# A two-layer hybrid encoder on one core: ScalarE, VectorE and GpSimd pinned to the written order in the attentions, with late work, straddling value blocks and fill rewritten

## The chip, the core and the metric

The kernel runs on one core of a Trainium2 chip. The metric is the device time of one execution in microseconds. A core has five engines that work side by side and meet at semaphores: TensorE (PE: matmuls and transposes into PSUM), VectorE (DVE), ScalarE (ACT), GpSimd (POOL) and SyncE (SP, which here issues all transfers). PEld stands for TensorE's weight loads.

## The reference

Two layers over 512 tokens (a grid of 8 rows by 64 columns) of width 1024, each with three residual parts, all in float32:

```python
x = x + hybrid_mixer(rms_norm(x, norm_mix[l]), ...)
x = x + memory_cross_attention(rms_norm(x, norm_mem_q[l]), rms_norm(mem, norm_mem_kv[l]), ...)
x = x + conv_ffn(rms_norm(x, norm_ffn[l]), ...)
```

The mixer projects its input once into two groups of heads of width 64. Eight heads do neighbourhood attention (NA) in a window of 8 rows by 16 columns with a learned relative bias. Eight query heads with two key-value heads do grouped attention (GQA) over all tokens, after a per-head RMS norm of q and k and an axial rotation. Both outputs go through one output projection. The memory attention has 4 heads of width 128 over 256 memory tokens. The feed-forward part is a SwiGLU (inner width 2816) with a depthwise convolution of width 3 over the positions. A last RMS norm closes the program.

## The kernel before

**Data.** Activations are kept transposed, 128 channels by 512 tokens (`xT`, eight chunks). Every operand of a large product is split into a high part `hi` and a rest `lo`, and a product is three matmuls (`mm3`). Weights arrive in float32 by SP (`emit_raw`, three buffers); ACT writes `hi` (L246) and POOL `lo` (L247), for up to three weights ahead of use, at the moment `get_w` asks for the next weight.

**Order.** The program is written in Tile. TensorE and SP are pinned to the order in which the program writes their instructions (`keep_in_program_order`, which ties an instruction to the one written before it on its engine). ACT, DVE and POOL are wrapped in `Free`, which passes calls through, so the order of their instructions is left to the framework's scheduler.

**Fill.** `weave` writes an attention as a software pipeline: in step s it writes the transposes of unit s-2, the normalise of unit s-1, the scores of unit s, and so on, and between them calls the filler. `Filler.run(ns)` adds `ns` to an account and takes the next pieces of a list of generators until their TensorE time (by a formula in `Counted.matmul`) has used it up. The list holds, in order: projections of the NA heads, of the GQA heads (`gqa_project`, order k, 0, 1, v, 2, 3), the NA half of the output projection (`out_na`), memory keys, memory values 0, and `close_rows("outg")`, the GQA half of the output projection, which has the memory values 1 as a generator `between`. A generator may yield a gate, a condition that must hold before it goes on; what is left at the end is written by `finish`. NA has 8 units (a pair of heads, half of the queries each) with three fills a step; GQA has 16 units with one fill a step.

**Late work.** `late(n, fn)` keeps `fn` until n ticks later. A tick comes after every filler piece, and also when a generator ends. So an eviction that needs time is written behind later matmuls.

**The rotary units.** After its projection each of k, 0, 1, 2, 3 is scaled and squared by ACT (L768, L769) and multiplied by the cosine table on DVE (L770). Two ticks later `rotate` writes four transfers that swap rows, POOL's product and sum (L775, L776), TensorE's sums of squares into a `tr` bank, DVE's scaling (L781, L783) and POOL's power and copy (L784, L785). Three ticks later `norm` spreads the factors by TensorE (`mm<-ident,t`), multiplies on DVE (L792) and splits the result (ACT L620, DVE L622). `gqa_v` turns v by four transposes (`turn`) two ticks after its projection.

**The other lines.** `split_psum` evicts a bank as `hi` (ACT L441) and `lo` (DVE L442). POOL normalises the exponentials (L448) with DVE's reciprocal (L825 in GQA); ACT's exponentials are L674 and L819, DVE's maxima L817. NA's values are folded by L718 to L720 and split by `split_out` (ACT L463, POOL L464) into `parts[0..3]`; GQA's values are folded by `fold` (ACT L455, DVE L457, then ACT L458 and POOL L459) into `parts[4..7]`, and `whole[i]` opens the gates of `close_rows`. `mem_stat` and `memory_prepare` write the memory's statistics (DVE L504) and operands (ACT L488, DVE L489) at the start of some GQA steps. `project_v` also writes value blocks that straddle two token blocks, by two ACT copies for each of three blocks (L642, L643). PSUM has four `mm`, two `sc` and two `tr` banks.

## Time and profile before

| | us |
|---|---|
| three runs | 1452.25, 1452.06, 1448.22 (median 1452.06) |
| the profiled execution, its own time | 1450.3 |
| its span from the first to the last instruction | 1448.4 |
| TensorE busy | 1375.9 |
| VectorE / ScalarE / GpSimd busy | 846.3 / 720.1 / 706.3 |
| mean granted TensorE clock | 0.977 |

How to read the profile: an instruction has the line of `kernel.py` that wrote it; pinned instructions have the line of the helper (L76 for matmuls, L63 for transposes and transfers). A tile's name stands without its number: `tr`, `sc` and `mm` are PSUM banks, `r` the general operand buffers, `t` temporary tiles, `xg` the large operand pair, `raw`, `hi`, `lo` weights. "x8" counts instructions. A wait is named by what ended last before the waiting instruction. By the timeline, layer 0's NA steps run to about 158 us, its GQA steps to about 280, its memory attention to about 360; layer 1's GQA steps run from about 867 to 987 and its memory attention to about 1060.

### The profile page before, as it was taken

Reading aid. Unit: us, or ns where it says so; the run is one execution under the profiler, and the core shown is the slowest. Engines: PE = TensorE matmul, PEld = TensorE weight load, DVE = VectorE, ACT = ScalarE, POOL = GpSimd, SP = SyncE. Lnnn points to the kernel's source line nnn. Section 1 sums busy time; section 2 is a strip of 40 time slices with the busy share of each in tenths; the row PEclk is TensorE's granted clock in tenths of the full one; section 3 lists DMA queues with packets and bytes.
Section 4 is the critical chain, followed back from the end, with each engine's and each line's share of the span. In section 5 each row is a group of like instructions: output and inputs, shape, how many; then the busy total and the mean of one; then the engine's idle time right before and its main releaser. Section 6 shows DMA issues by size and latency. Waiting matters only on the chain. (4 is left out here: it accounts for less than half of the span.)

```text
span 1448.4 us, 19205 instructions
## 1 busy us (share of the span) xinstructions
PE 1375.9 (95%) x7092; PEld 1173.4 (81%) x7092; DVE 846.3 (58%) x1437; ACT 720.1 (50%) x1332; POOL 706.3 (49%) x509
## 2 busy tenths in 40 slices
PE   7998799899999999999999987989899999999997
PEld 6987689677888888888888876987788888888897
DVE  5666566446488258448446646754637862871874
ACT  5785557556444234324557754756554432431441
POOL 2457547453544444444645655646254444444451
PEclk8999899899999999999999998999999999999998
DMA  7353212221333333332354432222223333333321
GB/s 231 117 140 94 73 44 74 71 75 53 94 95 96 102 93 91 104 104 81 106 151 140 109 90 68 69 59 88 58 59 107 97 102 92 96 89 105 96 77 59
DMA packets 216573, 135.68 MB, mean 94 GB/s; under 512 B 5664, under 2 KB 210720, under 8 KB 216480
## 3 DMA queue, kind: packets, MB, share of 16 engines
q1 hardware_dynamic: 216480, 134.46, 32.1%
q8 instruction: 56, 0.92, 0.3%
q14 instruction: 37, 0.30, 0.1%
HBM read 125.00 MB, written 2.10 MB: 88 GB/s over the span
## 5 line engine op out<-in xcount | busy, mean ns | idle before, releaser
L247 POOL TENSOR_TENSOR lo<-raw,hi 128x1024 fp32r<-128x1024 f32 (+2 forms) x268 | 500.2, 1878 | 575.0 <-ACT hi L246 558.7
L76 PE MATMUL mm<-xg,hi 128*128 128x512 f32 x1984 | 620.7, 394 | 1.9 <-ACT xg L63 1.5
L76 PEld LDWEIGHTS mm<-xg,hi 128*128 128x128 f32 x1984 | 372.8, 190 | 77.9 <-ACT xg L63 1.9
L246 ACT CAST hi<-raw 128x512 fp32r<-128x512 f32 (+2 forms) x276 | 224.1, 836 | 338.7 <-PE mm L76 290.5
L76 PE MATMUL mm<-xg,lo 128*128 128x512 f32 x992 | 388.7, 392 | 0.0
L76 PE MATMUL mm<-r,hi 128*128 128x512 f32 (+1 forms) x1160 | 341.3, 378 | 15.7 <-ACT r L458 12.1
L76 PEld LDWEIGHTS mm<-r,hi 128*128 128x128 f32 x1160 | 213.4, 191 | 57.5 <-ACT r L458 12.9
L1096 DVE SCALAR_TENSOR_TENSOR t<-t,par,t 128x7 f32<-128x7 f32 (+1 forms) x352 | 203.9, 647 | 34.0 <-ACT t L1089 34.0
L76 PEld LDWEIGHTS mm<-xg,lo 128*128 128x128 f32 x992 | 188.1, 190 | 40.3 <-DVE lo L247 0.4
L76 PE MATMUL mm<-r,lo 128*128 128x512 f32 (+1 forms) x580 | 217.9, 376 | 0.0
L76 PEld LDWEIGHTS mm<-r,lo 128*128 128x128 f32 x580 | 110.4, 190 | 19.3
L448 POOL TENSOR_SCALAR t<-t,s 128x512 f32<-128x512 f32 (+1 forms) x112 | 66.3, 607 | 97.2 <-DVE s L825 59.1
L1081 DVE TENSOR_TENSOR t<-mm,rep 128x512 f32<-128x512 f32 x88 | 60.2, 687 | 77.6 <-PE mm L76 62.3
L1098 ACT ACTIVATE t<-t 128x512 f32<-128x512 f32 x44 | 27.9, 633 | 138.9 <-DVE t L1096 138.9
L1102 DVE TENSOR_TENSOR r<-t,r 128x512 fp32r<-128x512 f32 x44 | 90.4, 2055 | 7.3 <-ACT r L1101 4.1
L1125 DVE TENSOR_TENSOR xT<-xT,mm 128x512 f32<-128x512 f32 x32 | 21.9, 686 | 106.7 <-PE mm L76 106.7
L63 PE MATMUL tr<-ident,t 128*128 128x128 f32 x456 | 65.5, 284 | 17.1 <-DVE r L442 11.5
L76 PE MATMUL sc<-r,r 128*128 128x256 f32 (+1 forms) x352 | 74.8, 345 | 3.4 <-DVE r L442 1.8
L63 PEld LDWEIGHTS tr<-ident,t 128*128 128x128 f32 x456 | 55.8, 147 | 23.5 <-issue 17.1
L1089 ACT ACTIVATE t<-t,par 128x512 f32<-128x512 f32 x88 | 66.8, 806 | 2.4 <-DVE t L1081 2.4
L76 PE MATMUL mm<-r,r 128*128 128x256 f32 (+1 forms) x428 | 62.2, 297 | 0.0
L76 PEld LDWEIGHTS sc<-r,r 128*128 128x128 f32 x352 | 53.6, 196 | 9.6 <-ACT r L441 3.0
(135 smaller groups left out, 1551.9 us busy)
## 6 DMA issues: line engine op xcount, KB each, us to landing
raw<-in_w_up SPq DMA_DIRECT2D x88, 512.0 KB, 3.9
raw<-in_w_in SPq DMA_DIRECT2D x34, 512.0 KB, 4.5
raw<-in_w_down SPq DMA_DIRECT2D x32, 448.0 KB, 3.9
raw<-in_w_mem_kv SPq DMA_DIRECT2D x16, 512.0 KB, 3.8
raw<-in_w_down SPq DMA_DIRECT2D x16, 512.0 KB, 4.2
r<-in_bias SPq DMA_DIRECT2D x16, 384.0 KB, 5.2
r<-r SPq DMA_DIRECT2D x18, 256.0 KB, 3.7
raw<-in_w_out SPq DMA_DIRECT2D x8, 512.0 KB, 3.8
```

Source lines behind the costliest of these rows:

```text
L63: return lambda *a, **k: self.tc.keep_in_program_order(op(*a, **k))
L76: return self.tc.keep_in_program_order(self.engine.matmul(out, lhsT, rhs, **k))
L246: act.copy(hi[:, k], raw[:, k])
L247: (POOL if eng[0] == "P" else DVE).tensor_sub(lo[:, k], raw[:, k], f(hi)[:, k])
L448: eng.tensor_scalar(e, e, sums[:, col : col + 1], 1.0, op0=ALU.mult, op1=ALU.mult)
L1081: DVE.tensor_mul(u, us[side], ffn.rep)
L1089: ACT.activation(cc, u, AF.Identity, bias=par[:, l, CB + ch : CB + ch + 1], scale=w[1])
L1096: DVE.scalar_tensor_tensor(cc[:, dst], u[:, src], wi, cc[:, dst], op0=ALU.mult, op1=ALU.add)
L1098: ACT.activation(cs[0], cs[0], AF.Silu)
L1102: DVE.tensor_sub(acts[j][1], cs[0], f(acts[j][0]))
L1125: DVE.tensor_add(xT[m], xT[m], pm)
```

## The change

- `Free` becomes `Switched`: while `ordered[0]` holds, every instruction of ACT, DVE and POOL is pinned to the written order as well. The switch is off at the start of layer 0, turned on after the first fill pieces there (in layer 1 from the layer's start), and off again before each feed-forward part.
- `Filler.run` ticks once when it finds the gate closed, and `finish` ticks until the gates open.
- `fold` and `split_out` write their last two instructions one tick later, and `whole` or `parts` is set then; `out_na` waits for `parts[3]`.
- `rotate` is cut in two: `swap`, one tick after the projection (transfers, sums of squares, DVE's scaling), and `rotate`, one tick later (POOL: power, copy, product, sum); `norm` follows two ticks after that.
- The straddling blocks of v are written by five transfers on SP for each half of v, two ticks after its last block, in place of twelve ACT copies a layer.
- `close_rows` writes the first of memory values 1 ahead of the gate of the third chunk, and the rest behind the gate of the last chunk. Memory values 1 splits one weight less ahead.
- The GQA fill is 2300 in sixteen steps and 3000 in the last four.

```diff
--- before.py
+++ after.py
@@ -46,7 +46,7 @@
 
 
 NA_FILL = 2650
-GQA_FILL = [2950] * 16 + [3000, 3000, 3000, 2900]
+GQA_FILL = [2300] * 16 + [3000] * 4
 MEM_FILL = [1, 1, 1, 2, 1, 0, 0, 2, 0, 1, 2]
 MEM_STEPS = [1, 0, 1, 1, 1, 1, 1, 1, 1] + [0] * 11
 N_RAW, N_W, AHEAD, AHEAD_HELD, N_WARM, N_LATE, N_FIRST = 3, 4, 2, 5, 10, 4, 3
@@ -76,14 +76,18 @@
         return self.tc.keep_in_program_order(self.engine.matmul(out, lhsT, rhs, **k))
 
 
-class Free:
-
-
-    def __init__(self, engine):
-        self.engine = engine
+class Switched:
+
+
+
+    def __init__(self, tc, engine, ordered):
+        self.tc, self.engine, self.ordered = tc, engine, ordered
 
     def __getattr__(self, name):
-        return getattr(self.engine, name)
+        op = getattr(self.engine, name)
+        if self.ordered[0]:
+            return lambda *a, **k: self.tc.keep_in_program_order(op(*a, **k))
+        return op
 
 
 class PartsView:
@@ -141,14 +145,18 @@
 
     def run(self, ns):
         self.owed += ns
+        if self.closed():
+            self.late.tick()
         while self.owed > 0 and not self.closed():
             t = self.pe.ns
             self.step(1)
             self.owed -= self.pe.ns - t
 
     def finish(self):
-        self.step(1 << 30)
-        assert not self.gens
+        while self.gens:
+            assert not self.closed() or self.late.todo
+            self.late.tick()
+            self.step(1 << 30)
         self.late.flush()
 
 
@@ -171,7 +179,8 @@
     PE, SP = Counted(tc, nc.tensor), InOrder(tc, nc.sync)
     late = Late()
     ACT_IN_ORDER = InOrder(tc, nc.scalar)
-    ACT, DVE, POOL = Free(nc.scalar), Free(nc.vector), Free(nc.gpsimd)
+    ordered = [False]
+    ACT, DVE, POOL = [Switched(tc, e, ordered) for e in (nc.scalar, nc.vector, nc.gpsimd)]
 
     cpool = ctx.enter_context(tc.tile_pool(name="cpool", bufs=1))
     xpool = ctx.enter_context(tc.tile_pool(name="xpool", bufs=1))
@@ -247,10 +256,10 @@
             (POOL if eng[0] == "P" else DVE).tensor_sub(lo[:, k], raw[:, k], f(hi)[:, k])
         ready.append((hi, lo))
 
-    def get_w(key):
+    def get_w(key, ahead=AHEAD):
         n = done[0]
         assert plan[n][0] == key, (plan[n][0], key)
-        ahead = n + 1 + AHEAD
+        ahead = n + 1 + ahead
         while ahead < min(len(plan), n + 1 + AHEAD_HELD) and plan[ahead][4][1:] == "r":
             ahead += 1
         while len(ready) < min(len(plan), ahead):
@@ -447,7 +456,7 @@
     def normalise(e, sums, col, eng=DVE):
         eng.tensor_scalar(e, e, sums[:, col : col + 1], 1.0, op0=ALU.mult, op1=ALU.mult)
 
-    def fold(out, po, cs):
+    def fold(out, po, cs, done):
 
         th, o32 = tmp((2, 256)), tmp((256,))
         rows = [slice(64 * j, 64 * j + 64) for j in range(2)]
@@ -455,8 +464,13 @@
             ACT.copy(th[r, j], po[64:128, j])
         for j, r in enumerate(rows):
             DVE.tensor_add(o32[r], po[0:64, j], th[r, j])
-        ACT.copy(out[0][:, cs], o32)
-        POOL.tensor_sub(out[1][:, cs], o32, f(out[0][:, cs]))
+
+        def split():
+            ACT.copy(out[0][:, cs], o32)
+            POOL.tensor_sub(out[1][:, cs], o32, f(out[0][:, cs]))
+            done()
+
+        late(1, split)
 
     def split_out(o32):
         hi, lo = rpair()
@@ -637,11 +651,19 @@
                     mm3(pm, xg[k][0][:, bs], xg[k][1][:, bs], wh, wl, k == 0, k == KC - 1)
                 v = vblk[g][P * b]
                 split_psum(v[:, :, 0:HD], v[:, :, HD:P], pm.rearrange("p (h d) -> p h d", d=HD), mix.rstd[:, b : b + 1])
-                if b > 0:
-                    o = vblk[g][P * b - 64]
-                    ACT.copy(o[0:64], vblk[g][P * b - P][64:128])
-                    ACT.copy(o[64:128], v[0:64])
+                if b == NB - 1:
+                    late(2, lambda: straddle(vs))
                 yield
+
+        def straddle(vs):
+            for dst, src in (
+                (vs[2][0:64, 0:2], vs[0][64:128, 0:2]),
+                (vs[2][64:128, 0], vs[0][0:64, 1]),
+                (vs[2][64:128, 1], vs[1][0:64, 0]),
+                (vs[3][0:64, 0], vs[1][64:128, 0]),
+                (vs[3][64:128, 0], vs[1][0:64, 1]),
+            ):
+                SP.dma_start(f(dst), f(src))
 
 
         na = {}
@@ -719,7 +741,7 @@
                 DVE.tensor_add(tt[r], po[0:64], th[r])
             DVE.tensor_add(o32s[p][:, 256 * bp : 256 * bp + 256].rearrange("p (i q) -> p i q", i=2), tt[:, :, 0], tt[:, :, 1])
             if bp == 1:
-                parts[p] = split_out(o32s.pop(p))
+                late(1, lambda: parts.__setitem__(p, split_out(o32s.pop(p))))
                 bias[p] = None
                 del qk["q", p], qk["k", p]
                 if p % 2 == 1:
@@ -769,21 +791,26 @@
             ACT.activation(sq, pm, AF.Square)
             DVE.scalar_tensor_tensor(cc, pm, gain, gtab[0][:, 0], op0=ALU.mult, op1=ALU.mult)
 
-            def rotate():
+            def swap():
                 for i in range(4):
                     SP.dma_start(xr[32 * i : 32 * i + 32], xs[32 * (i ^ 1) : 32 * (i ^ 1) + 32])
-                POOL.tensor_mul(xr, xr, gtab[0][:, 1])
-                POOL.tensor_add(xr, cc, xr)
                 pv = ps_t()
                 for b in range(NB):
                     PE.matmul(pv[:, 2 * b : 2 * b + 2], sq[:, b * P : (b + 1) * P], pairs, start=True, stop=True)
-                v, r = small(2 * NB), small(2 * NB)
+                v = small(2 * NB)
                 DVE.tensor_tensor(v.rearrange("p (b j) -> p b j", j=2), pv[:, 0 : 2 * NB].rearrange("p (b j) -> p b j", j=2),
                                   r2[0].unsqueeze(2).to_broadcast([P, NB, 2]), op=ALU.mult)
+
                 DVE.tensor_scalar(v, v, *((1.0 / HD, EPS) if g == "k" else (1.0, EPS * HD)), op0=ALU.mult, op1=ALU.add)
+                late(1, lambda: rotate(v))
+
+            def rotate(v):
+                r = small(2 * NB)
                 POOL.tensor_tensor(r, v, mhalf[:, : 2 * NB], op=ALU.pow)
                 POOL.tensor_copy(sq.rearrange("p (b d) -> p b d", d=HD), r.unsqueeze(2).to_broadcast([P, 2 * NB, HD]))
-                late(3, norm)
+                POOL.tensor_mul(xr, xr, gtab[0][:, 1])
+                POOL.tensor_add(xr, cc, xr)
+                late(2, norm)
 
             def norm():
                 pr = ps_mm()
@@ -797,7 +824,7 @@
                     gq[g] = rtile((2, S))
                     split_q(pr, gq[g])
 
-            late(2, rotate)
+            late(1, swap)
 
 
         ga, gpt = {}, {}
@@ -859,10 +886,10 @@
             del gpo[u], gpt[u // 2]
             if bp == 0:
                 parts[4 + i] = rpair()
-            fold(parts[4 + i], po, slice(256 * bp, 256 * bp + 256))
-            whole[i] = bp == 1
+            fold(parts[4 + i], po, slice(256 * bp, 256 * bp + 256), lambda: whole.__setitem__(i, bp == 1))
 
         def out_na():
+            yield lambda: parts[3] is not None
             for m in range(KC):
                 if m % 2 == 0:
                     w = get_w(("outn", m // 2))
@@ -885,12 +912,15 @@
                 rows.append((ps_mm(), w[m // 2], slice(P * (m % 2), P * (m % 2) + P)))
                 gemm_T(*rows[m][:2], ops, range(2), 0, 3, rows[m][2])
                 yield
+            for _ in range(len(between) and 1):
+                next(between[0])
+                yield
             yield lambda: ready(2)
             for pm, ws, c in rows:
                 gemm_T(pm, ws, ops, [2], 0, 3, c)
+            yield lambda: ready(3)
             for gen in between:
                 yield from gen
-            yield lambda: ready(3)
             norm = norm()
             for m in range(KC):
                 if m < n:
@@ -922,7 +952,7 @@
         def memory_values(g):
             if g == 0:
                 memv.extend(rpair() for _ in range(MB))
-            w = [get_w(("memv", g, kh)) for kh in range(2)]
+            w = [get_w(("memv", g, kh), AHEAD - g) for kh in range(2)]
             for b in range(MB):
                 pm = ps_mm()[:, :256]
                 bs = slice(b * P, b * P + P)
@@ -935,6 +965,7 @@
 
         if l > 0:
             load_bias(0)
+        ordered[0] = l > 0
         units = [project_v(p) if n == "v" else project_qk(n, p) for n, p in NA_ORDER]
         nns = []
         attn_fill = Filler(
@@ -943,6 +974,7 @@
             close_rows("outg", 2, PartsView(parts, 4), lambda k: whole[k], lambda: nns.append(Norm(G_MQ, l)) or nns[0],
                        memory_values(1)))
         attn_fill.step(N_FIRST if l == 0 else N_FIRST + 5)
+        ordered[0] = True
 
         def na_quanta(s):
             if s == 3:
@@ -1046,6 +1078,7 @@
         fill.finish()
 
 
+        ordered[0] = False
         ffn = nn
         acts = {}
 
```

## The prediction

> **What bounds the kernel now.** I read the page first, then who TensorE waited for, then TensorE's timeline at each wait, then the same microseconds on every engine. The profiled execution took 1450.3 us (span 1448.4 and 1.9 around it), 1.8 below the median of 1452.06; the sum below is made against 1450.3. About 0.3% (4.4 us) is what a measurement of this kernel can tell from no change.

> ```profile
> PE 1375.9 (95%) x7092; PEld 1173.4 (81%) x7092; DVE 846.3 (58%) x1437; ACT 720.1 (50%) x1332; POOL 706.3 (49%) x509
> ...
> PE   7998799899999999999999987989899999999997
> ...
> PEclk8999899899999999999999998999999999999998
> ```

> TensorE is the bound: the kernel can only gain where it stands still or runs at a low clock. Both happen in the same slices, 4 to 9 and 23 to 28, which are the attentions of the two layers; the feed-forward part is full.

> ```profile
> PE mm L76 <- ACT r L458: 12.1, 4, 3.8
> PE tr L63 <- DVE r L442: 11.5, 2, 5.8
> ...
> PE tr L76 <- DVE s L825: 6.8, 1, 6.8
> PE mm L76 <- POOL t L785: 6.4, 3, 3.7
> PE tr L63 <- DVE s L825: 4.7, 1, 4.7
> ```

> Columns: total us, times, longest. Two places per layer hold nearly all of it. The **tail** of the grouped attention (L458, the folded output): idle 3.85+0.26+0.34+2.21 = 6.7 us in layer 0 and 7.3 in layer 1. The **transition** from the neighbourhood attention to the grouped one (L442, L785, L825): 0.79+5.76+1.01+2.48+6.76+0.39 = 17.2 in layer 0, 0.47+5.75+0.20+3.70+4.74 = 14.9 in layer 1.

> ```profile
> 145.00:184.00 39.00, 28.74 (x134) 24.00 (x133) 23.05 (x37) 18.96 (x38) 21.89 (x20) 0.85 0.28 79
> 184.00:257.00 73.00, 72.56 (x480) 66.15 (x480) 48.39 (x94) 51.06 (x119) 44.11 (x50) 0.98 0.22 63
> 257.00:283.00 26.00, 19.32 (x111) 16.54 (x110) 7.94 (x16) 10.36 (x24) 8.56 (x9) 0.80 0.18 52
> ```

> Windows of layer 0 (start:end, length, busy of PE, PEld, DVE, ACT, POOL, then the granted clock): transition, steady grouped attention, tail. The steady part is full at 5.6 us a step (transposes at 214.96, 220.58, 226.22), so the tail is idle only because its fill was spent earlier.

> The transition's longest wait, all engines:

> ```profile
> 136.11 2.54 POOL L247 TENSOR_TENSOR lo<-raw,hi 128x512 fp32r<-128x512 f32 x2
> ...
> 138.60 1.26 POOL L776 TENSOR_TENSOR t<-t,t 128x512 f32<-128x512 f32 x1
> ...
> 140.54 0.69 DVE L792 TENSOR_TENSOR mm<-t,mm 128x512 f32<-128x512 f32 x1
> 141.27 1.17 ACT L620 CAST r<-mm 64x512 fp32r<-64x512 f32 x2 [1.93 <-DVE mm L792]
> ...
> 142.47 1.39 DVE L622 TENSOR_TENSOR r<-mm,r 64x512 fp32r<-64x512 f32 x2 [1.24 <-ACT r L620]
> 143.89 1.29 DVE L442 TENSOR_TENSOR r<-tr,r 128x512 fp32r<-128x512 f32 x2
> ...
> 144.73 1.09 PE L63 MATMUL tr<-ident,t 128*128 128x128 f32 x4 [5.76 <-DVE r L442]
> ```

> A transpose waits for a `tr` buffer, which DVE empties only after the rotary product L792, which waits for POOL's add L776, which stood behind a weight split (L247). The chain starts at POOL. After a wait TensorE is also slow: from 144.73 four transposes and twelve matmuls take 5.6 us, against 3.1 later, so 2.5 us lost; after the 2.48 wait 1.6, after 6.76 2.0. Layer 1 likewise: 2.5, 1.7, 1.2. Clock in the transitions: 11.5 us. In the tail, six matmuls from 261.04 take 3.1 us against 1.37, and again from 279.75: 3.4 lost; layer 1 some 1.8.

> **Part 1, the tail.** Walking the filler's account through the code (227 ns for a 512-column matmul, 120 for 256) shows steps 17 and 18 of the old grouped weave without fill, as the trace has it. With 2300 a step the fill reaches the end: step 16 holds the second block of memory values 0, step 17 two first halves of `outg` rows, step 18 a block of memory values 1, step 19 the third chunk of the rows; then the last block (24 matmuls, 2.88 us) stands between the last fold and the closing rows. The fold's chain is 2.95 us in the trace (L455 at 275.22 to the end of L459 at 278.14); over it now lie 1.36+2.88 = 4.2 us. The fill is only moved: the earlier steps shorten to about 5.0 us. Removed: 6.7+3.4+7.3+1.8 = 19.2; I leave 0.5 a layer, so 18.2. If the cover were gone it would cost 2.2 again in each layer.

> **Part 2, the transition.** DVE, ACT and POOL now run in the written order. A rotary unit (5 a layer) costs POOL power 1.65, copy 0.61, product 1.29, sum 1.28 = 4.8 us, a weight split 2.54, a normalise 1.4. From the split written with unit 0 to the first grouped transpose POOL has 5x2.54 + 2.54 for the first `outn` + 4x4.8 + 1.3 for each of three outputs + 4x1.4 = about 44 to 50 us (by whether the first rotary unit's end counts); TensorE has 49 us there. Both are full, so each wait in the fixed order shows. I lay the new order out by hand with these rows:
> - The statistics of a unit are now written right at the next fill call, and its squares (ACT L768 0.69, L769 0.59) must be ready: 1.35 us after the projection, behind a 0.9 us piece: 0.45 wait once; for unit 2 nothing lies between: 1.4.
> - The norm of unit 1 comes one half projection after its rotation was written. POOL has in front of it the split of v's weights and `split_out` (2.54+1.3): the copy is about 3.0 late (0.45 for unit 0).
> - The transpose after `turn` waits for L442 behind L622, as before, but POOL's four operations are now together: about 1.5 instead of 5.8.
> - At the first grouped step the written order is: scores 0, norm of unit 2, split of output 3, statistics of unit 3, rotation of unit 3, weights, `outn` half, normalise 0, scores 1, `outn` half, norm of unit 3, transposes 0. ACT reaches the split of output 3 only after two exponentials (0.69 each) that wait for DVE's L770 and maxima, and after L620 (1.18): about 5.4 us after scores 0. The second `outn` half waits 1.7 for it, norm 3 waits 1.7 for POOL's copy, and the transposes wait for POOL's 1.3+4.8+2.5+1.4 = 10 us, of which TensorE covers half: 5.0.

> Sum 0.45+0.45+3.0+1.5+1.4+1.7+1.7+5.0 = 15.2 a layer, 30.4 in both, clock (1.6+2.3 a layer) 7.8: 38.2 against 32.1+11.5 = 43.6. Gain 5.4. Next late is POOL. Bounds: 3 us of waits a layer (POOL never idle) to 20; I take the laid-out value, which is nearest to the 17.2 and 14.9 of now. DVE's memory reductions (2.06 each, part of the old 6.76) fall into the 5.0 wait and cost nothing; without it they would cost up to 2.5.

> **Part 3, the shorter steps.** ACT is busy 39.2 of 52 us from 198 to 250, DVE 37.0, POOL 31.6. At 5.0 instead of 5.6 us a step this is 85%, 80% and 68%: still room, but POOL's normalise now stands behind the weight split of the step before, and steps with one short `outn` half (4.2 us) leave no slack. I take 1 us in each of three such steps: +3 a layer, 6 in both. Bounds 0 and 20.

> A row that bears on this: the memory operands' L489 (two a step, written ahead of the transposes in four steps a layer) has a median of 0.475 us, but five of its sixteen took 0.87 to 1.49, each beside a POOL instruction; 3.2 us of DVE in all, off the path, so I add nothing. [...]

> **Part 4, at nothing.** Twelve ACT copies a layer at 0.62 become ten transfers (about 0.6 us of issue each on SP, 128 to 256 KB). The first reader comes some 9 us of TensorE work later; the 256 KB copies among `r` tiles land in 3.7 us (the page's median), five in a row, 0.6 apart, in about 6.5 (an estimate from these rows). Behind them on SP stand weight loads three ahead, and the swap. If the cover were gone: up to 3 us each. ACT's 7.4 us a layer lie where TensorE is full. The memory attention (idle 4.2 us a layer) is pinned but not rewritten: 0, bounds -1 and +3 a layer.

> **Sum.** 1450.3 - 18.2 - 5.4 + 6 = 1432.7, say 1433; its own range 1418 to 1445 (part 2 with 11 to 18 us of waits a layer, part 3 with 0 to 12 in both).

> **Rivals.** (a) **The transition clears**: POOL runs without holes and the waits fall to 3 a layer, no new ones in the steady steps. For it: POOL stood 11 us idle inside the old stall (139.9 to 151.0). Against: the hand-laid order has two holes of 4 to 5 us. Waits 6 instead of 30.4, clock 0, steady 0: 1433 - 24 - 8 - 6 = 1395. (b) **The pinned queues cost more than they give, slower**: in the grouped steps POOL's normalise (L448) queues behind the weight split (2.54) with about 0.9 of slack, so 1.7 us in each of some ten steps a layer that write a split, 34 in all instead of 6: 1433 + 28 = 1461. It decides from 23.6 us, the gain of parts 1 and 2, which is 0.7 us in each of the 32 grouped steps. For it: ACT at 85%; against: the split falls into the fill, which is longest just there (2.88). [...] (c) **No net effect**: the transition at its upper bound (20 of waits and 5 of clock a layer, +12) and three more slow steps a layer (+6) take back what the tail gives: 1433 + 18 = 1451.

> **Numbers.** Forecast 0.53, (a) 0.24, (b) 0.15, (c) 0.08. Faster is the forecast and (a), 0.77; same takes most of (c), 0.07; slower 0.16. The range 1392 to 1458 leaves out the far half of (a) and of (b), some 0.1 each.

> **What would show it.** Right: no wait of the closing rows for the last folded output over 0.5 us, step length about 5.0 up to the end; a wait of about 5 us of the first grouped transposes for POOL's normalise; no 5.8 us wait for L442. (a): those are gone as well. (b): waits for the normalise of 1 to 2 us spread over the grouped steps, clock dips inside them. Wrong: idle TensorE in the neighbourhood steps before the first rotary unit (ACT or DVE blocked behind a weight's landing or a straddling block), or in the memory attention above 5 us a layer.

## The result and the profile after

The changed kernel takes 1514.66 us (median of 1508.98 to 1517.57) against 1452.12 us for the kernel before on the same chip. The ratio is 1.0431, with a 95% interval of 1.0412 to 1.045: slower by 62.5 us, where 1433 us and a gain were forecast. The time lies 57 us above the upper end of the range. The profiled execution took 1517.57 us (span 1515.8).

The page first: busy time of the engines, then PE and the granted clock in 40 slices.

```profile
PE 1407.5 (93%) x7092; PEld 1190.1 (79%) x7092; DVE 848.5 (56%) x1437; ACT 705.4 (47%) x1308; POOL 705.2 (47%) x509
...
PE   8988889897999999999999978989799999999997
...
PEclk9998999998999999999999988999989999999998
```

TensorE has the same 7092 matmuls as before, but is busy 31.6 us longer (1407.5 against 1375.9) and idle 35.8 us longer (108.3 against 72.5). The sum, 67.4, is the difference of the spans. So about half of the loss is waiting. Most of the other half is the low clock behind the waits: the mean granted clock is 0.961 over 1515.8 us against 0.977 over 1448.4, which makes some 26 us more lost to the clock; the remaining 6 us of longer busy time are not accounted for. The loss lies in the attentions: the last stretch, from layer 1's feed-forward part to the end, takes 358 us in both.

From the first and last score matmul of each attention, the stages of layer 0 compare so (layer 1 in brackets): first neighbourhood score to first grouped score 113.9 to 133.0 us (113.8 to 133.3); grouped scores 98.2 to 95.1 (95.7 to 92.2); last grouped score to first memory score 60.7 to 62.9 (59.3 to 61.9); memory scores 21.5 to 30.7 (21.5 to 30.5); last memory score to the feed-forward part 46.9 to 53.5 (46.7 to 53.5). The loss is in the neighbourhood stage with the transition, and in the memory attention.

Whom TensorE waited for (total us, times, longest), to be read beside the five rows of before:

```profile
PE tr L63 <- POOL t L89: 25.8, 14, 3.2
PE tr L63 <- DVE t L89: 21.4, 8, 4.5
PE tr L63 <- DVE s L89: 11.2, 2, 5.6
PE mm L76 <- POOL t L89: 7.1, 2, 3.6
PE tr L76 <- DVE r L89: 7.0, 4, 1.8
PE tr L76 <- ACT t L89: 3.5, 4, 1.3
PE mm L76 <- POOL lo L89: 3.3, 4, 1.4
```

L89 is the helper that keeps an instruction in order, so every ordered instruction has this line. The row of the folded output (12.1 us) is gone. In its place the closing rows wait 1.4 us a layer for a weight's low part (the last row above, longest 1.4). The two large new rows, 25.8 and 21.4 us, are transposes that wait for a normalise, by GpSimd in the mixing attentions and by VectorE in the memory attention. I show four of these waits.

**Memory attention, 4.48 us.** All engines, layer 0 (start, us, then idle time before it and its releaser):

```profile
352.05 0.46 ACT L89 ACTIVATE t<-sc,s 128x256 f32<-128x256 f32 x1
...
352.50 0.58 ACT L89 CAST r<-mm 128x512 fp32r<-128x512 f32 x1
353.11 0.69 DVE L89 TENSOR_TENSOR r<-mm,r 128x512 fp32r<-128x512 f32 x1 [1.56 <-ACT r L89]
353.72 0.69 DVE L89 SCALAR_TENSOR_TENSOR mm<-mm,rep 128x512 f32<-128x512 f32 x1
354.44 0.58 ACT L89 CAST r<-mm 128x512 fp32r<-128x512 f32 x1 [1.36 <-DVE mm L89]
354.93 0.59 ACT L89 CAST r<-tr 128x512 fp32r<-128x512 f32 x1
355.06 0.69 DVE L89 TENSOR_TENSOR r<-mm,r 128x512 fp32r<-128x512 f32 x1 [0.65 <-ACT r L89]
355.67 0.68 DVE L89 TENSOR_TENSOR r<-tr,r 128x512 fp32r<-128x512 f32 x1
356.27 0.15 DVE L89 RECIPROCAL s<-s 128x2 f32<-128x2 f32 x1
356.46 0.62 DVE L89 TENSOR_SCALAR t<-t,s 128x256 f32<-128x256 f32 x2
356.96 0.66 PE L63 MATMUL tr<-ident,t 128*128 128x128 f32 x2 [4.48 <-DVE t L89]
```

Before, for the same unit (the fifth), TensorE waited 0.19 us:

```profile
332.48 0.15 DVE L1005 RECIPROCAL s<-s 128x2 f32<-128x2 f32 x1
332.67 0.62 DVE L448 TENSOR_SCALAR t<-t,s 128x256 f32<-128x256 f32 x2
...
333.17 0.63 PE L63 MATMUL tr<-ident,t 128*128 128x128 f32 x4 [0.19 <-DVE t L448]
...
333.81 0.68 DVE L442 TENSOR_TENSOR r<-tr,r 128x512 fp32r<-128x512 f32 x1
```

In the changed kernel the exponentials end by 352.6, so the reciprocal could run then. It stands behind two low parts from `mm`, a query's scaling and the transposes' low part. Two of these wait for a cast by ScalarE, and one of the casts waits for VectorE's scaling. The two engines hand the work back and forth until 356.27, while TensorE stands still.

**Neighbourhood attention, 3.24 us.** GpSimd and, in the last line, TensorE:

```profile
79.89 2.49 POOL L89 TENSOR_TENSOR r<-r,rep 128x512 f32<-128x512 f32 x2 [14.48 <-DMA r<-in_rope]
82.33 0.21 POOL L89 TENSOR_TENSOR s<-s 128x4 f32<-128x4 f32 x1
82.50 1.64 POOL L89 TENSOR_SCALAR t<-t,s 128x256 f32<-128x256 f32 x3
```

```profile
83.29 0.93 PE L63 MATMUL tr<-ident,t 128*128 128x128 f32 x3 [3.24 <-POOL t L89]
```

The product of the rope table is written right behind its load (issue at 73.3, landing 6.5 us later). It isn't needed until the first rotary unit, but the normalise behind it is, and GpSimd stands idle for 14.5 us in front of both.

**Statistics, 1.84 us and what comes behind.** TensorE, layer 0:

```profile
110.02 1.64 PE L76 MATMUL tr<-pairs,t 128*128 128x2 f32 x8 [1.84 <-DVE r L89]
111.52 1.20 PE L76 MATMUL mm<-xg,hi 128*128 128x512 f32 x2
```

```profile
111.00:119.00 8.00, 8.00 (x33) 6.84 (x33) 2.12 (x8) 0.63 (x3) 7.86 (x8) 0.62 0.67 174
```

The second fence is the window from 111 to 119 (length, busy of PE, PEld, DVE, ACT and POOL, then the granted clock): TensorE is busy all of it at a granted clock of 0.62, so it loses 8.00 x 0.38 = 3.0 us, more than the wait itself.

**The turn, 5.61 us** (before: 5.76). The releaser has changed:

```profile
142.57 0.69 DVE L89 TENSOR_TENSOR mm<-t,mm 128x512 f32<-128x512 f32 x1
143.34 1.17 ACT L89 CAST r<-mm 64x512 fp32r<-64x512 f32 x2 [6.51 <-DVE mm L89]
...
144.55 1.39 DVE L89 TENSOR_TENSOR r<-mm,r 64x512 fp32r<-64x512 f32 x2 [1.29 <-ACT r L89]
...
145.95 0.17 DVE L89 TENSOR_TENSOR s<-tr,s 128x8 f32<-128x8 f32 x1
...
146.26 1.09 PE L63 MATMUL tr<-ident,t 128*128 128x128 f32 x4 [5.61 <-DVE s L89]
```

The statistics of the next unit hold a transpose buffer, and VectorE empties it (0.17 us) only behind the rotary product and its two low parts, which wait for ScalarE.

### The profile page after: what moved, and what is told of

Same layout as the page of the kernel before. It is cut to its first block, busy times and chain, and to the rows that moved or that the text cites. A ratio compares the mean times of both kernels' runs of the same rounds, so it can differ in the third digit from the quotient of the medians.

```text
span 1515.8 us, 19254 instructions
## 1 busy us (share of the span) xinstructions
PE 1407.5 (93%) x7092; PEld 1190.1 (79%) x7092; DVE 848.5 (56%) x1437; ACT 705.4 (47%) x1308; POOL 705.2 (47%) x509
## 4 chain that ended last, share of the span: by engine, by line
PE 69%; DVE 10%; ACT 9%; issue 5%; POOL 4%; DMA 1%; SPq 0%; DVEq 0%; POOLq 0%; ACTq 0%
PE mm L76 65%; ACT t L89 4%; DVE xg L89 2%; ACT r L89 2%; DVE r L89 2%; DVE t L89 2%; POOL t L89 2%; PE tr L63 2%; PE sc L76 1%; DVE s L89 1%; PE tr L76 1%; ACT hi L89 1%; ACT xg L89 1%; DVE mm L89 1%; POOL lo L89 1%
## 5 line engine op out<-in xcount | busy, mean ns | idle before, releaser
L76 PE MATMUL mm<-xg,hi 128*128 128x512 f32 x1984 | 629.8, 399 | 4.5 <-ACT xg L63 2.6
L256 POOL TENSOR_TENSOR lo<-raw,hi 128x1024 fp32r<-128x1024 f32 (+2 forms) x134 | 305.7, 2284 | 378.7 <-ACT hi L255 378.6
L76 PEld LDWEIGHTS mm<-xg,hi 128*128 128x128 f32 x1984 | 377.0, 192 | 83.6 <-ACT xg L63 3.0
L76 PE MATMUL mm<-xg,lo 128*128 128x512 f32 x992 | 393.0, 396 | 0.0
L76 PE MATMUL mm<-r,hi 128*128 128x512 f32 (+1 forms) x1160 | 340.1, 378 | 1.3 <-ACT hi L89 1.1
L89 POOL TENSOR_TENSOR lo<-raw,hi 128x512 fp32r<-128x512 f32 (+1 forms) x134 | 193.9, 1469 | 196.3 <-ACT hi L89 193.3
L255 ACT CAST hi<-raw 128x1024 fp32r<-128x1024 f32 (+2 forms) x136 | 134.8, 996 | 268.1 <-PE mm L76 261.9
L76 PEld LDWEIGHTS mm<-r,hi 128*128 128x128 f32 x1160 | 213.9, 192 | 40.2 <-ACT hi L89 1.9
L76 PEld LDWEIGHTS mm<-xg,lo 128*128 128x128 f32 x992 | 190.6, 192 | 41.7 <-DVE lo L256 0.9
L76 PE MATMUL mm<-r,lo 128*128 128x512 f32 (+1 forms) x580 | 218.2, 376 | 2.8 <-POOL lo L89 2.8
L89 ACT ACTIVATE t<-sc,s 128x256 f32<-128x256 f32 (+1 forms) x160 | 87.8, 556 | 116.4 <-DVE s L89 107.1
L63 PE MATMUL tr<-ident,t 128*128 128x128 f32 x456 | 73.7, 297 | 61.3 <-POOL t L89 25.8
L76 PEld LDWEIGHTS mm<-r,lo 128*128 128x128 f32 x580 | 110.7, 191 | 23.4 <-POOL lo L89 3.7
L63 PEld LDWEIGHTS tr<-ident,t 128*128 128x128 f32 x456 | 55.2, 150 | 79.5 <-issue 37.4
L89 POOL TENSOR_SCALAR t<-t,s 128x512 f32<-128x512 f32 (+1 forms) x112 | 66.1, 605 | 87.3 <-DVE s L89 84.4
L89 ACT CAST hi<-raw 128x512 fp32r<-128x512 f32 (+1 forms) x140 | 88.1, 683 | 6.2 <-PE mm L76 5.7
L76 PE MATMUL sc<-r,r 128*128 128x256 f32 (+1 forms) x352 | 78.5, 358 | 2.5 <-ACT r L89 1.3
```

Of the source, the lines that this page charges most:

```text
L63: return lambda *a, **k: self.tc.keep_in_program_order(op(*a, **k))
L76: return self.tc.keep_in_program_order(self.engine.matmul(out, lhsT, rhs, **k))
L89: return lambda *a, **k: self.tc.keep_in_program_order(op(*a, **k))
L255: act.copy(hi[:, k], raw[:, k])
L256: (POOL if eng[0] == "P" else DVE).tensor_sub(lo[:, k], raw[:, k], f(hi)[:, k])
```

## The experiments

My theory P: the fixed order of the three engines is the loss. Rival R: the rewritten order of the late work, or the transfers, is the loss. Each run is a median of four or more, with the ratio to the kernel before on the same chip; that kernel's median lay between 1450.5 and 1451.7 us beside e1 to e19.

| run | us | ratio, 95% interval |
|---|---|---|
| changed kernel | 1514.7 | 1.0412 to 1.045 |
| e1 no fixed order | 1452.5 | 0.9992 to 1.0014 |
| e3 memory attention free | 1486.4 | 1.0227 to 1.0258 |
| e4 rope table early | 1508.1 | 1.0376 to 1.0407 |
| e5 before, tail alone | 1431.5 | 0.9849 to 0.9878 |
| e6 e5 and transfers | 1432.6 | 0.9856 to 0.9886 |
| e7 e1, one-piece rotary work | 1428.8 | 0.9831 to 0.9861 |
| e8 VectorE alone ordered | 1517.7 | 1.0424 to 1.0475 |
| e9 GpSimd alone ordered | 1444.2 | 0.9934 to 0.9966 |
| e10 ScalarE alone ordered | 1469.6 | 1.0112 to 1.016 |
| e16 VectorE alone free | 1463.4 | 1.0073 to 1.0103 |
| e11 e9, one-piece rotary work | 1459.2 | 1.0041 to 1.0071 |
| e12 all ordered, one-piece | 1535.6 | 1.0543 to 1.0578 |
| e13 memory normalise first | 1495.6 | 1.0286 to 1.0317 |
| e14 grouped normalise first too | 1501.4 | 1.0339 to 1.037 |
| e15 e14, rope early, statistics later | 1478.7 | 1.0184 to 1.0216 |
| e17 e7, memory statistics later | 1429.5 | 0.9838 to 0.9871 |
| e18 e9, rope early, statistics later | 1421.6 | 0.9765 to 0.9815 |
| e19 e18 with all three free | 1412.7 | 0.9715 to 0.9759 |

**The order off, and the parts alone.** e1 takes the order off everywhere:

```diff
-        ordered[0] = l > 0
-        ordered[0] = True
-        ordered[0] = False
```

> The changed kernel with the fixed order of ScalarE, VectorE and GpSimd taken off everywhere; the later writing of late work, the transfers for straddling blocks and the refilled end stay. Theory P (the fixed order is the loss: instructions that could run stand behind ones that wait): the extra waits of the neighbourhood stage and of the memory attention go, the shorter tail stays, so the kernel before less the 15 to 18 us of the tail: 1430 to 1440 us, idle TensorE about 55 to 60 us instead of 108. Rival R (the rewritten order of late work or the transfers on SP's queue are the loss): it stays above 1490 us.

Measured 1452.5: neither. The order costs 62 us, but the rest of the change, which holds the tail, is worth nothing either. e5 gives only the tail to the kernel before (`GQA_FILL`, `close_rows`, `get_w` and the filler's tick as in the change):

> The kernel before with only the end refilled: shorter fill in the first sixteen grouped steps, longer in the last four, one block of memory values ahead of the third chunk, closing rows ready in that order. Theory P and the prediction's part 1: waits in the tail from 6.7 and 7.3 us to under 1 a layer, clock of the tail full: 1452 - 18 = 1434 us. Rival S (the fill taken from the grouped steps is missed there, the steps stop being full): the gain is given back, 1445 to 1455 us.

1431.5, as theory P and part 1 have it: 20.0 us. So 21 us were lost in e1 by something else. e6 adds the ten transfers to e5, by `straddle` in place of the two ScalarE copies a block:

> The kernel before with the refilled end (1431.5 us alone) and the straddling blocks of v by ten transfers a layer in place of twelve copies on ScalarE; order free, late work as before. The run without fixed order lost 21 us against the refilled end alone, with these transfers and the later-written work both in it. Theory T (later-written work is what costs): the transfers cost nothing, 1429 to 1434 us. Rival U (the transfers' place on SP's queue delays the loads of the neighbourhood stage): most of the 21 us, 1445 to 1453 us.

1432.6, theory T: the difference of 1.2 us can't be told from none. e7 is e1 with the rotary units' late work as before:

```diff
-            late(1, swap)          # statistics; then rotate 1, norm 2 calls later
+            late(2, rotate)        # all in one piece; then norm 3 calls later
```

> The changed kernel without fixed order, and with the rotary units' late work as in the kernel before (transfers, statistics and GpSimd's four operations in one piece two fill calls after the projection, norm three later); the later splits of the folded outputs and of the neighbourhood outputs, the gates, transfers and end of the change stay. Theory T1 (statistics written at the very next fill call wait for ScalarE's squares: 13.1 us of TensorE waits in the run without fixed order, and half-speed stretches behind them): 1432 to 1438 us. Rival T2 (the later splits or the gate ahead of the first output rows move work into the neighbourhood stage): stays at 1447 to 1453 us.

1428.8: T1, and 3 us below its range. The split rotary work costs 23.7 us in a free order, and the other later splits and gates nothing. In e1's waits the new row is the one of the squares, which before is not among the first ten rows; the second row here is the wait for a rotary unit's GpSimd copy:

```profile
PE tr L76 <- ACT t L791: 13.1, 8, 2.5
PE mm L76 <- POOL t L810: 10.9, 2, 6.3
```

e3 moves the switch back, so that the memory attention alone is free:

```diff
         attn_fill.finish()
+        ordered[0] = False
         nn = nns[0]
```

> The changed kernel with the fixed order switched off before the memory attention instead of after it. Theory P: memory attention back to 4 us idle a layer and its scores back to 21.5 us from first to last (30.7 in the changed kernel), 9.1 and 6.7 us a layer less: 1514.7 - 2 x 15.8 = 1483 us. Rival R: the memory attention is late because of what stands ahead of it (weight landings, the late fill), so the order doesn't matter there: 1510 to 1517 us.

1486.4, theory P; the memory scores span 21.6 us again, and the free VectorE takes the reciprocal and the normalise first:

```profile
337.37 0.15 DVE L1038 RECIPROCAL s<-s 128x2 f32<-128x2 f32 x1
337.56 0.62 DVE L457 TENSOR_SCALAR t<-t,s 128x256 f32<-128x256 f32 x2
...
338.69 0.68 DVE L451 TENSOR_TENSOR r<-mm,r 128x512 fp32r<-128x512 f32 x1
...
339.29 0.68 DVE L451 TENSOR_TENSOR r<-tr,r 128x512 fp32r<-128x512 f32 x1
```

The low parts come 1.3 us behind, when ScalarE's casts are ready. Order in the memory attention costs 28.3 us, and in the mixing attentions the 34 us between e3 and e1.

These runs put the whole of it in one line: 1451.5 - 20.0 (tail) + 1.2 (transfers) - 3.9 (other late work) + 23.7 (split rotary work) + 33.8 (order, mixing attentions) + 28.3 (order, memory attention) = 1514.6. The terms depend on the sequence in which they are put: the split costs 23.7 without order, but with it saves 21 (e12 below).

**Which engine's order.** The switch is given to one engine, the others stay free (e16: to the other two):

```diff
-    ACT, DVE, POOL = [Switched(tc, e, ordered) for e in (nc.scalar, nc.vector, nc.gpsimd)]
+    free = [False]
+    ACT, DVE, POOL = [Switched(tc, e, o) for e, o in zip((nc.scalar, nc.vector, nc.gpsimd), (free, ordered, free))]
```

> The changed kernel with only VectorE in the program's order through the attentions. All three in order cost 62 us over none (1514.7 against 1452.5). If VectorE's queue is the chief one (the low-part subtractions that wait for ScalarE stand ahead of reciprocal and normalise in the memory attention, and the turn's subtraction stands behind the rotary product): 1485 to 1500 us, the memory scores again 30 us from first to last. If the engines' orders only hurt together: 1452 to 1465 us.

> The changed kernel with only GpSimd in the program's order. By the changed kernel's waits GpSimd releases 36 us of them against 13 without fixed order; with the slow stretches behind them some 30 us: 1475 to 1485 us, memory scores at 21.5 us from first to last (it does little there). If GpSimd was late only because VectorE and ScalarE fed it late: under 1460 us.

> The changed kernel with only ScalarE in the program's order (VectorE alone gave 1517.7, GpSimd alone 1444.2, none 1452.5, all three 1514.7). If ScalarE's place is free in most stretches (busy 47% of the span), its order costs little: 1450 to 1460 us, memory scores within 23 us from first to last. If the weight casts and evictions that now stand ahead of exponentials hold them up by themselves: 1475 to 1490 us, memory scores 26 us or more.

> The changed kernel with VectorE alone out of order; ScalarE and GpSimd in order. None in order 1452.5; GpSimd took 8 off, ScalarE put 17 on. If VectorE's order is the cause: about 1452.5 - 8 + 17 = 1461, 1455 to 1470 us. If any two fixed orders already meet in the same waits: over 1480 us.

VectorE alone gives 1517.7, the whole loss and more than I expected; ScalarE alone 17 us (between my two cases); GpSimd alone saves 8, the second of my cases (it was late only because it was fed late); without VectorE's order 1463.4, as expected from the sum. The waits of e8 show why GpSimd had looked guilty:

```profile
PE tr L63 <- POOL t L458: 25.9, 11, 4.5
```

GpSimd (L458) is free here, and still TensorE waits 25.9 us for its normalise: in e8's trace, before the wait of 4.5 us, the reciprocal at 280.17 comes behind the two sums of a fold, a memory key's product and low part, and two low parts of transposes, and only then can GpSimd normalise. The releaser that the view names is the last of a chain; which engine holds it up is seen when one engine is freed at a time.

**The written order, with all engines still in order.** e4 and e13 change one place each, e14 and e15 add to it:

```diff
-            if s == 3:                                # e4, e15
+            if s == 0:
                 gtab.append(rtile((2, S), F32))
                 SP.dma_start(gtab[0], t["rope"])
+            if s == 3:
                 gqa_tables()
...
-  [(2, mem_transpose), (1, mem_normalise), ...      # e13 to e15
+  [(1, mem_normalise), (2, mem_transpose), ...
-  [(2, gqa_transpose_p), (1, gqa_normalise), ...    # e14, e15
+  [(1, gqa_normalise), (2, gqa_transpose_p), ...
-            late(1, swap)                             # e15
+            late(2, swap)
```

> The changed kernel with the load of the rope table written at step 0 of the neighbourhood attention and its product still at step 3. Theory D (GpSimd stands idle 14.5 us, of which 6.5 for this load, with a normalise queued behind the product): the 3.2 and 3.0 us waits at the neighbourhood transposes go, and the slow stretch after each (about 1.5): 1514.7 - 2 x 4.6 = 1505 us. Rival: GpSimd's own work in front of the normalise (two products of 1.3 us, a weight split of 2.5) is what is late, then the wait shrinks to 1 to 2 us: 1511 us. If the load is hidden anyway: 1515.

1508.1, a gain of 6.6 where 9 were expected: the 3.2 and 3.0 us waits are gone, but 0.75 us appears at the next matmuls.

> The changed kernel, with only the memory attention's steps written otherwise: the normalise of a unit ahead of the transposes of the one before, so that VectorE's reciprocal and normalise stand ahead of that transpose's low part. Theory Q (what costs in the memory attention is VectorE's normalise behind low parts that wait for ScalarE, not being in order as such): the two waits of 1.4 us go and the 4.5 us one shrinks to about 3, with their slow stretches some 5 us a layer: 1505 us. If the other low parts, those of the queries and values, hold it as well: 1511 to 1515 us.

1495.6: twice the expected gain. The row of VectorE's normalise falls from 21.4 to 11.3 us:

```profile
PE tr L63 <- DVE t L89: 11.3, 6, 3.9
```

An exchange of two neighbouring steps gives back 19 of the 28 us that order costs in the memory attention. So two thirds of that cost is the written order and not that it is fixed; the other 9 us stay open.

> All three engines in order as in the changed kernel; the normalise is written ahead of the transposes in the memory attention (as before: 1495.6 us) and now in the grouped attention too. Theory Q (VectorE's reciprocal stands behind low parts that wait for ScalarE, so GpSimd's normalise starts late): the 7.5 us a layer of steady waits for GpSimd's normalise go, with some 3 us of slow stretches: 1495.6 - 21 = 1475 us. Rival B (the normalise is late because it stands behind weight splits in GpSimd's own order, rival b of the prediction): 1492 to 1499 us.

1501.4, so this expectation failed: the same exchange in the grouped attention gains nothing, and the intervals of e13 and e14 lie apart, so it loses some. The result lies above the range of rival B too (1492 to 1499 us); GpSimd's own queue is left as the likely reason.

> The same as the run with normalise first in both attentions, and in addition the rope table loaded at step 0 and the rotary units' transfers and statistics written one fill call later. Theory W (the written order is what costs, being in order isn't): the load gave 6.6 us alone; the statistics' waits are 6 us a layer in the changed kernel and at least two of them are followed by a half-speed stretch of 2.5 us: 6.6 + 2 x (6 + 5) = 29 us less than that run. Rival (later statistics make GpSimd's rotary work late, and the wait comes back at the norms): at most 10 us less.

In e15, where the exchange is kept, GpSimd does this before a TensorE wait of 3.6 us:

```profile
257.87 5.01 POOL L89 TENSOR_TENSOR lo<-raw,hi 128x512 fp32r<-128x512 f32 x4
262.82 0.73 POOL L89 TENSOR_TENSOR r<-t,r 128x256 fp32r<-128x256 f32 x1
263.52 1.37 POOL L89 TENSOR_SCALAR t<-t,s 128x512 f32<-128x512 f32 x2
```

The sums were reciprocated at 260.1, but two weight splits of 2.5 us stand ahead of the normalise. This is rival (b)'s mechanism, seen in the trace, but no run takes it away. e15 took 1478.7: 22.7 less than e14 of the 29 expected, by the rope table and the later statistics.

> The changed kernel with GpSimd alone in order and the rotary units' late work in one piece as before. GpSimd's order took 8.3 us off the kernel without order, the one-piece rotary work 23.7. If the two add up: 1452.5 - 8.3 - 23.7 = 1420 us, and the 5.8 us wait of the turn's transposes (VectorE's subtraction behind the rotary product, which waits for GpSimd's sum) shrinks as it did from 4.25 to 1.05. Rival: GpSimd's order helps only the split work; in one piece its power waits at once for the statistics, and weight splits behind it come late: 1428 to 1440 us.

> The changed kernel, all three engines in order, with the rotary units' late work in one piece as before. If the cost of the order and that of the split rotary work add up: 1514.7 - 23.7 = 1491 us. Rival (the splitting was what the order needed: in one piece VectorE's statistics and rotary product stand in its queue while GpSimd works, and all its evictions behind them): 1514 us or more, longer waits at the transition.

e11 took 1459.2, beyond its rival, and e12 1535.6, its rival. In one piece, the rotary work blocks an ordered GpSimd. In e11:

```profile
117.62 1.26 POOL L89 TENSOR_TENSOR t<-t,r 128x512 f32<-128x512 f32 x1 [5.05 <-DVE s L703]
...
120.19 1.84 POOL L89 TENSOR_TENSOR s<-s,mhalf 128x8 f32<-128x8 f32 x1
...
122.68 1.38 POOL L89 TENSOR_SCALAR t<-t,s 128x256 f32<-128x256 f32 x3
```

GpSimd stands idle 5.05 us, and then four operations of the rotary unit run ahead of the normalise for which TensorE waits 8.4 us. So the split that I saw cost 24 us in a free order is what an ordered GpSimd needs (1444.2 against 1459.2).

**Versions that beat both kernels.** e17 moves the memory statistics of layer 0 one grouped step away from their sums (`MEM_STEPS` 1,0,1,0,1... in place of 1,0,1,1,1...; the list serves layer 1 as well, where it moves the memory operands):

> The version without fixed order and with one-piece rotary work (1428.8 us), and with the memory statistics of layer 0 written one grouped step later, away from the sums that they need. The wait of 7.6 us of those matmuls for VectorE (layer 0 only) and the slow stretch after it (about 2.5) go: 1419 us. Rival (the memory operands come a step later, the fill for the keys closes and the steps run empty, or the transposes wait in its place): 1427 to 1432 us.

1429.5 against 1428.8, the rival: the 7.6 us wait is gone, and 3.2, 2.0 and 2.2 us have come in the transposes behind it. e18 and e19 keep the split rotary work, with the statistics one fill call later and the rope table early; e18 has GpSimd in order, e19 nothing:

> The changed kernel with only GpSimd in order, the rope table loaded at step 0, and the rotary units' transfers and statistics written one fill call later. With GpSimd alone in order (1444.2) the statistics' waits are 2.8, 2.1, 0.7, 2.1 and 1.3 us in layer 0 and the same in layer 1: 9 us a layer, with half-speed stretches of about 2.5 us behind the three longest. If the place of the statistics is the cost: 1444 - 2 x (8 + 5) = 1418 us, below all others. If the split as such is (GpSimd's work then late for the norms): 1435 us or more.

> The same with all three engines free. Without order the split lost 23.7 us (1452.5 against 1428.8). If the place of the statistics is the cost: back to 1425 to 1432 us. If the split as such is: above 1442 us.

1421.6 and 1412.7. e18 is 3.6 us above the case for the place of the statistics; e19 is 12 us below its lower bound, and nothing here shows why it gained that much more. The cost of the split was the place of the statistics: one fill call later, the split is better than one piece by 16 us (e19 against e7). The early rope table is part of both edits, and no run without order separates it; but in e1, which loads it late, no TensorE wait over 0.15 us stands between 34 us and the first statistics at 109.5, nor in the same stretch of layer 1, so its share should be small. e19 is 0.9737 of the kernel before (0.9715 to 0.9759), and the best of all. Its page:

```profile
PE 1362.3 (97%) x7092; PEld 1162.8 (82%) x7092; DVE 844.9 (60%) x1437; ACT 704.9 (50%) x1308; POOL 703.9 (50%) x509
...
PEclk8999999999999999999999999999999999999999
```

Idle time is 47.9 us (1410.2 - 1362.3) against 72.5 before, TensorE is busy 13.6 us less for the same matmuls, and the clock row has lost its dips. The turn's wait of 5.8 us doesn't appear any more; one of 9.0 us remains, at the memory statistics of layer 0.

## Why the prediction was wrong, point by point

The step that failed is the price of the fixed order. The prediction took GpSimd for the engine that decides ("Next late is POOL"). It gave VectorE's fixed queue 1.5 us a layer at the turn and nothing in the memory attention. But VectorE's order alone gives the whole loss (e8, 1517.7 us), and GpSimd's saves 8 (e9). Parts 2, 3 and 4 came to +0.6 us in the prediction (-5.4 + 6 + 0). In the runs the same parts make 1.2 - 3.9 + 23.7 + 33.8 + 28.3 = 83.1. By part:

- **Part 1, the tail, was right.** 18.2 us forecast, 20.0 measured alone (e5). In the changed kernel 0.54 and 1.41 us stay in each layer, where 0.5 was left; both are for the two parts of a weight, so the cover was enough for the fold (its chain is 2.92 us, not 2.95) and not for the weight split.
- **Part 4, the transfers, was right** (e6). **Part 4, the memory attention "pinned but not rewritten: 0, bounds -1 and +3 a layer", failed outright:** 14.2 a layer (e3), a term put at nothing without a laid-out order. I had taken the order in which before.py is written for the order in which it ran. With free engines the scheduler had put the reciprocal and the normalise ahead of the low parts; the written order has them behind. To pin a stage is to rewrite it.
- **Part 2 laid out the wrong stretch.** The hand-laid order began at the weight split of unit 0, and so left out GpSimd's rope product four steps earlier and the loads it waits for (6.6 us, e4). "Idle TensorE in the neighbourhood steps before the first rotary unit" stood among the signs that would prove it wrong, and came, though with GpSimd blocked behind the rope table, not ScalarE or VectorE behind a weight.
- **Part 2, the statistics, was mis-sized.** The forecast 0.45 and 1.4 a layer came, as 0.43 and 1.32; but 1.84 and 1.69 came as well, ahead of k and unit 0. I priced the wait for the squares from the projection's end, but the transpose buffer is free later than that (the 1.84 and 1.69 are for VectorE's low part).
- **Part 2, the clock, was its largest mis-sized term.** The sum had 3.9 us a layer, behind two long waits, and nothing behind short ones. From 108.2 to 202 us the granted clock was 0.84, from 854.9 to 950 it was 0.87, which cost 13.8 and 10.2 us of TensorE's busy time; 3.0 of them stand behind the 1.84 us wait.
- **Part 2, the turn, had the right queue and the wrong occupant.** 1.5 us were forecast behind the low part; 5.61 came behind the rotary product, because the earlier statistics hold the buffer now. On the other hand the 5.0 us at the first grouped transposes came as 0.5, and the 3.0 at the norm of unit 1 didn't come, while the norm of unit 3 waited 3.55 for GpSimd's copy where 1.7 were forecast. All waits from 108 to 196 us make 19.4 a layer against 15.2 forecast.
- **Part 3 was mis-sized.** 3 us a layer forecast, 7.5 and 7.3 measured as waits for GpSimd's normalise. The longest of each layer (3.19 and 3.20) stands in a step without fill, since 2.88 us blocks had overdrawn the 2300 ns quanta; the one of 2.08 stands in a step with a short `outn` half, as forecast, and the others in full steps.
- **Rival (b) had the right sign and the wrong place.** The grouped steps hold 14.8 us of waits in both layers; the engine that decides was VectorE, which no rival priced.
- **Rival (a)**, a transition that clears, is nearest to e19, which has two things that the change didn't have: free engines, and statistics one call later. The turn's wait is gone there, but 9.0 us stay at the memory statistics, and it lies 18 us above the 1395 forecast for the rival.

## What to carry to other kernels

Before fixing an engine's order, compare the written order with the order that ran, stage by stage: each instruction that had moved ahead can become a wait. Fix one engine at a time, and lay out its written order over the whole stretch that is fixed. A short matmul that needs an evicted buffer or a fresh elementwise result is written one independent block later, not at the next opportunity.

## What the runs showed of the hardware

**The clock.** A wait's cost doesn't follow its length alone. In the changed kernel a wait of 2.08 us at 218.7 and those of 1.45 and 1.38 us in the memory attention had a granted clock of 1.00 behind them. The 1.84 us wait ahead of eight matmuls of two columns was followed by the 3.0 us loss shown above, the one of 1.32 us ahead of eight such matmuls by a clock of 0.61 from 166 to 169, and the 4.48 us wait by 0.50 from 357 to 360. In e19 a wait of 1.38 us ahead of eight small matmuls had 1.00 behind it, so it doesn't always come.

```profile
106.87:110.29 3.42, 1.58 (x13) 1.21 (x12) 2.26 (x5) 2.89 (x6) 0.31 (x2) 1.00 0.52 152
110.29:113.70 3.41, 3.41 (x12) 3.02 (x13) 1.28 (x4) 1.31 (x3) 3.41 (x3) 0.50 1.07 250
113.70:117.11 3.41, 3.41 (x10) 2.64 (x10) 0.00 (x0) 0.00 (x0) 3.35 (x4) 0.50 0.73 215
117.11:120.52 3.41, 3.41 (x24) 3.12 (x24) 1.86 (x8) 1.55 (x7) 2.96 (x5) 1.00 0.02 6
```

I counted, over all traces but for their ends, how much of each step at full clock was filled by matmuls of 128 columns or more. Below 43% the next step was at 0.50 in 266 of 266 cases, above 70% in none of 7603, and between them in 38 of 234, which stay open; in the traces of the two kernels alone these are 34 of 34, none of 754 and 4 of 23. The steps of the 1.84, 1.32 and 4.48 us waits were filled to 38%, 34% and 0%. Those of the 1.45 and 1.38 us waits in the memory attention were filled to 58 and 60%. The 2.08 us wait and the one in e19 are each divided between two steps (75 and 63%, 57 and 76%). If the matmuls of two columns are counted too, the 1.32 us wait's step is at 61%, so they seem to count for little.

The 38% and 34% show that a step doesn't have to be wholly idle for the next one to be at 0.50.

**VectorE beside GpSimd.** Of the 32 normalises of 128x256 that VectorE does in the memory attentions of the changed kernel, 28 took 0.34 to 0.36 us, and none of these ran beside a GpSimd instruction. The four that began while GpSimd ran a weight split of 128x1024 took 1.26 to 1.28 us and ended 0.15 us after the split. Why they took longer is not shown. Part 3 had seen such long ones in L489 alone (0.87 to 1.49 us against a median of 0.475) and added nothing for them.
